# Loading x first and summing the modulation on TensorE in the opening phase of a hybrid decoder layer

## The chip, the cores and the metric

The kernel runs on one core of a Trainium2 chip. The metric is the time of one execution on the device in microseconds (us); smaller is better. The engines are named as in the profile: PE (TensorE matmuls) with PEld (its weight loads), DVE (VectorE), ACT (ScalarE), POOL (GpSimd) and SP (SyncE, which issues the DMAs here).

## The reference, cut to what matters

One layer of a decoder: a mixing sub-layer (pooling channels and dilated window attention) and a gated MLP, both modulated by a conditioning vector `c`. SEQ and D_MODEL are 1024, one sequence, all in f32. The change concerns the very first part: the norm of `x`, its modulation by the first 2048 columns of `c_act @ w_ada` (shift and scale), and the start of the input projection.

```python
c_act = jax.nn.silu(c)
mod = c_act @ w_ada[l] + b_ada[l]
sh_m, sc_m, gt_m, sh_f, sc_f, gt_f = (t[:, None, :] for t in jnp.split(mod, N_MOD, axis=-1))
h = rms_norm(x, g_pre_mix[l]) * (1.0 + sc_m) + sh_m
y = mixing_sublayer(h, cos, sin, w_in[l], w_pool[l], b_pool[l], pool_scale[l], w_out[l])
...
# in mixing_sublayer
proj = h @ w_in
...
q = partial_rope(qkv[:, :, 0], cos, sin) * (HEAD_DIM ** -0.5)
```

`cos` and `sin` come from the token positions.

## The kernel before, in words

`x` lies in eight tiles `xt[0]` to `xt[7]` of 128 tokens by 1024 features. The projection needs h with the features on the partitions, so h is made in eight chunks of 128 features: `turn` (L356) transposes one chunk of the tiles into the PSUM banks 6 and 7, and `h_chunk` (L404) applies scale and shift as per-partition columns while it copies them out on ACT. A product in f32 is made of three matmuls of reduced width: `hh` is the high part of h, `hl` the low part (`low`, L410), `wh` and `wl` those of a weight piece (`piece`, with `split` at L118 and L170). `proj(kc, 0)` is the high part of h times both parts of the weights (L399, L400), `proj(kc, 1)` the low part times the high weights (L396). In this first phase six of the eight token tiles (`NS`) go through the projection of the first attention unit chunk by chunk, each with a PSUM bank of its own; the last two tiles follow together (`turn_rest` L367, `h_rest` L374, `l_rest` L382).

The modulation columns of chunk kc come from a block `wa[kc]` of `w_ada`, 128 x 8 x 256 in f32, 1 MB. `mods` on DVE multiplies its eight 256-wide parts by the eight columns of `cact` and adds them up, two running sums in `acc` (L335 the first products, L339 the multiply-adds, L342 the sum of the two). `colsum` (L346) sums over the partitions on PE: two matmuls with `acc` as weights and a column of ones. `columns` (L350, L352) turns the result into the columns `acol` and `bcol`.

The norm: `norm_a` squares a tile with its sum on ACT (L315) and takes the root (L147), `norm_b` refines it and scales the tile in place (L325 on DVE; L323 on ACT for the tiles in `ON_ACT`). `angles` makes the angles on DVE and the sines on ACT (L243, L244). `warm` issues matmuls of a matrix of ones into a spare bank (L361).

The order on PE, ACT, DVE and POOL is written out by hand in this phase (`manual_schedule`): each engine runs its instructions in the order of the calls. The DMAs go out on SP in the order of `START`, as far as `loads` is called: a is a block of modulation weights, x a tile, w a weight piece of the first unit, i the identity and other early constants, m the masks. `wa` has three buffers, weight pieces two (`raw`), `acc` two. Before the loop, the modulation of block 0 and the norm of the first six tiles are done, in pairs (`NB`). Step kc of the loop over chunks 1 to 7 transposes chunk kc, sums its modulation over the partitions, prepares that of kc + 1 on DVE, makes h of chunk kc and projects chunk kc - 1. The norm of tiles 6 and 7 stands in step `NRM` = 6. After this phase only PE's order is written by hand; ACT's and DVE's is the scheduler's, which has put two weight pieces of the next unit into step 6.

Of the kernel before, what the change touches and what calls it, by code (L numbers as in the profile page):

```python
# [19 lines left out]
NK = D // P  # L20
# [50 lines left out]
NCONST = _const_layout()  # L71
LAST_X = (8, 6)
TURN_AT = ((5, 4, 0, 0), (6, 2, 0, 1), (6, 7, 1, 0), (7, 2, 1, 1), (8, 3, 2, 0), (8, 7, 2, 1), (9, 7, 3, 0), (10, 3, 3, 1))
START = "a0 x0 i0 x1 x2 x3 x4 x5 w0 a1 w1 a2 a3 w2 a4 a5 w3 a6 a7 x6 x7 m0"
WARM = (5, 5, 5)
NB = 2
NRM = 6
RT = 3
SPL = 3
MU = 2  # L80
# [19 lines left out]
def block_kernel(ctx: ExitStack, tc: tile.TileContext, x, pos, cols, rows, consts, w_ada_a, w_ada_b, w_in_u,  # L100
                 w_in_p, w_pool, w_out, w_up, w_down, out):
    nc = tc.nc
# [42 lines left out]
    def root(ssq, n=1, scale=1.0 / D):  # L145
        sd = sp.tile([P, n], F32, name="sd", tag="sm_sd")
        nc.scalar.activation(sd, ssq, AF.Sqrt, bias=epst, scale=scale)  # L147
        return sd
# [19 lines left out]
    def split(raw, wh, wl, hi_eng=None, lo_eng=None):  # L168
        copy(hi_eng or nc.scalar, wh, raw)
        (lo_eng or nc.vector).tensor_tensor(wl, raw, wh.bitcast(F32), ALU.subtract)  # L170
# [63 lines left out]
    def angles():  # L234
        nc.vector.tensor_copy(posf, posi)
        nc.vector.tensor_tensor(ang, posf[:, :, None].to_broadcast([P, NT, 8]),
                                cl("freq")[:, None, :].to_broadcast([P, NT, 8]), ALU.mult)
        nc.vector.tensor_scalar(turns, ang, INV_2PI, MAGIC, op0=ALU.mult, op1=ALU.add)
        nc.vector.tensor_scalar(turns, turns, MAGIC, None, op0=ALU.subtract)
        for part in _two_pi_parts():  # L240
            nc.vector.scalar_tensor_tensor(ang, turns, -part, ang, op0=ALU.mult, op1=ALU.add)
        nc.vector.tensor_scalar(ang, ang, 3.1415925, -3.1415925, op0=ALU.min, op1=ALU.max)
        nc.scalar.activation(sin, ang, AF.Sin)  # L243
        nc.scalar.activation(cos, ang, AF.Sin, scale=0.5)  # L244
        nc.vector.tensor_mul(cos, cos, cos)
        nc.vector.tensor_scalar(cos, cos, -2.0, 1.0, op0=ALU.mult, op1=ALU.add)

# [44 lines left out]
    with tc.tile_pool(name="st", bufs=2) as st:  # L292
        wa, raws = [], []

        def load(what, i):
            if what == "x":
                nc.sync.dma_start(xt[i], xv[:, i])
            elif what == "i":
                nc.sync.dma_start(cst[:, :early], consts[:, :early])
            elif what == "m":  # L300
                nc.sync.dma_start(cst[:, early:], consts[:, early:])
            elif what == "w":
                raws.append(load_raw(w_in_u[0, :, 2 * i:2 * i + 2, :], 768))
            else:
                w = st.tile([P, 8, 256], F32, name="wa", tag="wa", bufs=3)
                nc.sync.dma_start(w, w_ada_a[i])
                wa.append(w)

        ws, accs = [], {}
# [3 lines left out]
        def norm_a(t, n=1):  # L313
            for i in range(n):
                nc.scalar.activation(hl[7], xt[t + i], AF.Square, accum_out=ssq[:, t + i:t + i + 1])  # L315
            roots[t] = root(ssq[:, t:t + n], n)

        def norm_b(t, n=1):
            r0, v = rsqrt_parts(ssq[:, t:t + n], roots[t], n)
            for i in range(n):  # L320
                if (t, i) in ON_ACT:
                    nc.vector.tensor_scalar_mul(v[:, i:i + 1], v[:, i:i + 1], r0[:, i:i + 1])
                    nc.scalar.activation(xt[t + i], xt[t + i], AF.Copy, scale=v[:, i:i + 1])  # L323
                else:
                    nc.vector.tensor_scalar(xt[t + i], xt[t + i], r0[:, i:i + 1], v[:, i:i + 1], op0=ALU.mult,  # L325
                                            op1=ALU.mult)

        def mods(kc, part):
            if kc >= NK:
                return  # L330
            w = wa[kc]
            if part == 0:
                accs[kc] = st.tile([P, 2, 256], F32, name="acc", tag="acc", bufs=2)
                for i in range(2):
                    nc.vector.tensor_scalar_mul(accs[kc][:, i], w[:, 4 * i], cact[:, 4 * i:4 * i + 1])  # L335
            for j in ((1,), (2, 3))[part]:
                for i in range(2):
                    kb = 4 * i + j
                    nc.vector.scalar_tensor_tensor(accs[kc][:, i], w[:, kb], cact[:, kb:kb + 1], accs[kc][:, i],  # L339
                                                   op0=ALU.mult, op1=ALU.add)  # L340
            if part:
                nc.vector.tensor_add(accs[kc][:, 0], accs[kc][:, 0], accs[kc][:, 1])  # L342

        def colsum(kc):
            for i in range(2):
                nc.tensor.matmul(PS[:, 7, 256 + i:257 + i], accs[kc][:, 0, i * P:(i + 1) * P], ones[:, 0:1],  # L346
                                 start=True, stop=True)

        def columns(kc):
            nc.vector.tensor_scalar(acol[:, kc:kc + 1], PS[:, 7, 257:258], bsc1[:, kc:kc + 1], cl("g_pre_mix", kc),  # L350
                                    op0=ALU.add, op1=ALU.mult)
            nc.vector.tensor_add(bcol[:, kc:kc + 1], PS[:, 7, 256:257], cl("b_ada", kc))  # L352
# [29 lines left out]
                nc.vector.tensor_tensor(o[:, :, NS * P:], h32[:, i:i + n], hh[:, k:k + n, NS * P:].bitcast(F32),  # L382
                                        ALU.subtract)

        def piece(j):
            wh = wp.tile([P, 768], F32R, name="wh", tag="wh")
            wl = wp.tile([P, 768], F32R, name="wl", tag="wl")
            split(raws[j], wh, wl)
            ws.append((wh, wl))

        def proj(kc, part, ts_=range(NS)):
# [9 lines left out]

        def h_chunk(kc):
            h32 = st.tile([P, NS * P], F32, name="h32", tag="h32")
            nc.scalar.activation(h32, PS[:, 6:8, :].rearrange("p a b -> p (a b)")[:, 0:NS * P], AF.Identity,  # L404
                                 bias=bcol[:, kc:kc + 1], scale=acol[:, kc:kc + 1])
            copy(nc.scalar, hh[:, kc, 0:NS * P], h32)
            return h32

        def low(kc, h32):
# [2 lines left out]
        with tc.manual_schedule(engines={ET.PE, ET.Activation, ET.DVE, ET.Pool}):  # L412
            order = START.split()
            at = [0]

            def loads(n):
                for _ in range(n):
                    if at[0] < len(order):
                        load(order[at[0]][0], int(order[at[0]][1]))
                        at[0] += 1  # L420

            loads(order.index("a3"))
            angles()
            root(epst)
            for part in range(2):
                mods(0, part)
            colsum(0)
            for t in range(0, NS, NB):
                norm_a(t, NB)
                norm_b(t, NB)  # L430
                turn(0, range(t, t + NB))
                if t == 0:
                    columns(0)
                warm(WARM[t // 2])
            mods(1, 0)
            piece(0)
            h32 = h_chunk(0)
            mods(1, 1)
            low(0, h32)
            for kc in range(1, NK):  # L440
                loads((2, 3)[kc % 2])
                turn(kc, range(NS))
                if kc == 1:
                    proj(0, 0, range(SPL))
                colsum(kc)
                if kc == 1:
                    proj(0, 0, range(SPL, NS))
                mods(kc + 1, 0)
                columns(kc)
                if kc == NRM:  # L450
                    norm_a(NS, 2)
                h32 = h_chunk(kc)
                if kc > 1:
                    proj(kc - 1, 0)
                mods(kc + 1, 1)
                if kc == NRM:
                    norm_b(NS, 2)
                low(kc, h32)
                if kc in (1, 3, 5):
# [1003 lines left out]
```

## Time and profile before

| | us |
|---|---|
| median of 3 runs | 1079.86 (1079.12 to 1080.65) |
| the profiled execution | 1080.04 |
| its span, first to last instruction | 1078.3 |
| PE busy in the span | 1038.9 (96%) |
| DVE busy | 860.6 (80%) |
| ACT busy | 474.8 (44%) |
| mean granted TensorE clock | 0.99 |

The span is what the profile covers; the execution's own time has some 1.7 us around it. Busy shares are means over stages with different limits: the phase that is changed covers about the first 60 us.

### The profile page before, as it was taken

The numbers are of one execution on the slowest core, as the hardware profiler recorded it, in microseconds if no ns is written. First come the engines' busy times: TensorE is split into PE (matmuls) and PEld (weight loads), VectorE is DVE, ScalarE is ACT, GpSimd is POOL, SyncE is SP. The second block draws the span as 40 slices with busy tenths as digits, with TensorE's granted clock in tenths as the row PEclk, the third lists the DMA queues.
The fourth block names the chain that finished last, engine by engine and source line by source line (L and its number), as shares of the span: only waits on it lengthen the run. The fifth ranks groups of instructions, "written<-read, shape, count | busy, mean of one in ns | idle before, by whom it ended". The sixth has DMA issues, their size and how long they took to land.

```text
span 1078.3 us, 15477 instructions
## 1 busy us (share of the span) xinstructions
PE 1038.9 (96%) x5174; PEld 876.9 (81%) x5174; DVE 860.6 (80%) x1886; ACT 474.8 (44%) x958; POOL 217.9 (20%) x132
## 2 busy tenths in 40 slices
PE   4899999999999999999999999999999999999996
PEld 4898988898888877777888888888878888888885
DVE  8975466885457779999999888979789999756997
ACT  6564332433354469534433333432223455544541
POOL 0000000000000000063433333323235525003360
PEclk9999999999999999999999999999999999999999
DMA  9652346353131163323344424344434889566653
GB/s 361 212 154 74 114 112 193 94 174 91 53 94 51 30 235 137 118 88 131 120 160 140 164 100 155 118 150 163 166 117 138 287 290 383 161 196 207 225 173 117
DMA packets 85148, 168.34 MB, mean 156 GB/s; under 512 B 9158, under 2 KB 25926, under 8 KB 81356
## 3 DMA queue, kind: packets, MB, share of 16 engines
q1 hardware_dynamic: 85068, 167.35, 46.7%
q8 instruction: 41, 0.67, 0.3%
q14 instruction: 39, 0.32, 0.1%
HBM read 134.47 MB, written 32.84 MB: 155 GB/s over the span
## 4 chain that ended last, share of the span: by engine, by line
PE 73%; DVE 16%; DMA 5%; ACT 3%; issue 2%; SPq 0%; POOL 0%; DVEq 0%; ACTq 0%; POOLq 0%
PE PS L1044 9%; PE PS L1045 9%; PE PS L1046 9%; PE PS L1345 6%; PE PS L1344 6%; PE PS L1346 6%; PE PS L222 5%; PE PS L224 5%; PE PS L223 5%; PE PS L685 3%; PE PS L655 2%; DMA gm<-in_w_ada_b_dram 2%; DMA mraw<-in_w_ada_b_dram 2%; PE PS L675 1%; DVE more L1119 1%
## 5 line engine op out<-in xcount | busy, mean ns | idle before, releaser
L1123 POOL TENSOR_TENSOR raws<-rw 128x512 f32<-128x512 f32 x30 | 45.5, 1516 | 512.5 <-DVE t2r L1068 450.3
L222 PE MATMUL PS<-wh,hh 128*128 128x384 f32 x336 | 125.4, 373 | 0.0
L224 PE MATMUL PS<-wh,hl 128*128 128x384 f32 x336 | 113.9, 339 | 0.0
L223 PE MATMUL PS<-wl,hh 128*128 128x384 f32 x336 | 113.7, 338 | 0.0
L118 ACT ACTIVATE more<-raws 128x512 fp32r<-128x512 f32 x81 | 49.6, 624 | 67.0 <-PE PS L1045 53.1
L1119 DVE TENSOR_TENSOR more<-raws,more 128x512 fp32r<-128x512 f32 x75 | 71.7, 958 | 3.1 <-ACT more L118 3.1
L664 ACT ACTIVATE pm<-pm,nm 128x128 f32<-128x128 f32 (+1 forms) x96 | 42.4, 443 | 65.0 <-DVE nm L662 43.8
L222 PEld LDWEIGHTS PS<-wh,hh 128*128 128x128 f32 x336 | 64.0, 190 | 7.9 <-issue 4.8
L223 PEld LDWEIGHTS PS<-wl,hh 128*128 128x128 f32 x336 | 64.0, 191 | 0.6 <-issue 0.5
L224 PEld LDWEIGHTS PS<-wh,hl 128*128 128x128 f32 x336 | 63.7, 189 | 0.0
L1064 ACT ACTIVATE cv<-GG,col 128x1024 f32<-128x1024 f32 x22 | 27.4, 1245 | 76.0 <-DVE GG L1063 76.0
L1044 PE MATMUL PS<-a,more 128*128 128x512 f32 x144 | 56.1, 390 | 1.3 <-DVE VV L1060 1.3
L1046 PE MATMUL PS<-a,more 128*128 128x512 f32 x144 | 56.3, 391 | 1.0 <-DVE more L1119 1.0
L1045 PE MATMUL PS<-a,more 128*128 128x512 f32 x144 | 56.0, 389 | 0.0
L658 DVE CUSTOM_DVE_ANT_0 pm<-PS,cst 128x128 f32<-128x128 f32 (+1 forms) x96 | 30.8, 348 | 29.7 <-PE PS L655 22.6
L1345 PE MATMUL PS<-tail 128*128 128x512 f32 x128 | 49.9, 390 | 0.0
L1344 PE MATMUL PS<-tail 128*128 128x512 f32 x128 | 49.8, 389 | 0.0
L1346 PE MATMUL PS<-tail 128*128 128x512 f32 x128 | 49.8, 389 | 0.0
L1158 ACT ACTIVATE cv<-cv 128x1024 f32<-128x1024 f32 x22 | 23.4, 1062 | 57.9 <-DVE cv L1156 57.9
L1154 DVE SCALAR_TENSOR_TENSOR cv<-GG,col,cv 128x1023 f32<-128x1023 f32 x22 | 36.9, 1678 | 11.4 <-ACT cv L1064 11.4
L170 DVE TENSOR_TENSOR wl<-raw,wh 128x768 fp32r<-128x768 f32 (+1 forms) x34 | 34.8, 1033 | 12.0 <-ACT wh L118 11.8
L489 DVE SCALAR_TENSOR_TENSOR macc<-mraw,cact,macc 128x512 f32<-128x512 f32 x42 | 31.4, 748 | 15.6 <-DMA mraw<-in_w_ada_b_dram 15.4
(389 smaller groups left out, 3102.5 us busy)
## 6 DMA issues: line engine op xcount, KB each, us to landing
rw<-in_w_up_dram SPq DMA_DIRECT2D x21, 1024.0 KB
gscr<-VV SPq DMA_DIRECT2D x66, 256.0 KB
mraw<-in_w_ada_b_dram SPq DMA_DIRECT2D x48, 256.0 KB
R<-in_w_down_dram SPq DMA_DIRECT2D x48, 256.0 KB
raw<-in_w_in_u_dram SPq DMA_DIRECT2D x24, 384.0 KB
wa<-in_w_ada_a_dram SPq DMA_DIRECT2D x8, 1024.0 KB
R<-gscr SPq DMA_DIRECT2D x27, 256.0 KB
raws<-in_w_up_dram SPq DMA_DIRECT2D x25, 256.0 KB
```

What stands on the lines that cost most here:

```text
L118: nc.scalar.activation(o, i, AF.Copy)
L222: nc.tensor.matmul(o, a, wh[:, c0:c0 + 384], start=k == 0, stop=False)
L223: nc.tensor.matmul(o, a, wl[:, c0:c0 + 384], start=False, stop=False)
L224: nc.tensor.matmul(o, b, wh[:, c0:c0 + 384], start=False, stop=k == 7)
L1044: nc.tensor.matmul(o, wh[:, ks], ah, start=k == 0, stop=False)
L1045: nc.tensor.matmul(o, wh[:, ks], al, start=False, stop=False)
L1046: nc.tensor.matmul(o, wl[:, ks], ah, start=False, stop=k == 3)
L1119: nc.vector.tensor_tensor(wl, r, wh.bitcast(F32), ALU.subtract)
L1123: nc.gpsimd.tensor_tensor(t, a, b, ALU.add)
L1344: nc.tensor.matmul(o, gh[:, ts_], wh, start=k == 0, stop=False)
L1345: nc.tensor.matmul(o, gh[:, ts_], wl, start=False, stop=False)
L1346: nc.tensor.matmul(o, gl[:, ts_], wh, start=False, stop=k == KD - 1)
```

## The change

- `START`: the first x tile goes ahead of modulation block 0, which is now loaded in two halves behind the sixth x tile; tiles 6 and 7 move ahead of block 3. The first call loads 14 entries, each later step as many as `LOADS` says.
- `ON_PE` gives for each block how many of its eight parts are multiplied and summed on PE directly, with the block's 128 x 128 squares as weights and columns of `cact` as the moving operand. For block 0 it is all eight, and nothing is left on DVE; block 1 has four, block 2 two, block 4 four, the others none.
- `mods_first`: the two first products of what remains move from DVE to ACT (for block 1 they stay on DVE).
- Piece 0's high part is made on DVE, behind the columns of chunk 0. Chunk 0's `hh` is written straight from PSUM, ahead of `h32`.
- In step 1 the first half of the projection of chunk 0 stands ahead of the transposes.
- The norm of tiles 6 and 7 moves from step 6 to step 3, the sines (with ACT's table) from the start to step 5, the cosines on DVE with them. The third block of warm-up matmuls goes.

```diff
-START = "a0 x0 i0 x1 x2 x3 x4 x5 w0 a1 w1 a2 a3 w2 a4 a5 w3 a6 a7 x6 x7 m0"
-WARM = (5, 5, 5)
+START = "x0 i0 x1 x2 x3 x4 x5 a0 w0 a1 w1 a2 x6 x7 a3 w2 a4 w3 a5 a6 a7 m0"
+FIRST_LOADS, LOADS = 14, (0, 2, 2, 1, 1, 1, 1, 0)
+ON_PE = (8, 4, 2, 0, 4, 0, 0, 0)
+TRIG_AT = 5
+WARM = (5, 5, 0)
 NB = 2
-NRM = 6
+NRM = 3
...
+        def mods_first(kc, eng):
+            if kc >= NK or ON_PE[kc] == 8:
+                return
+            accs[kc] = st.tile([P, 2, 256], F32, name="acc", tag="acc", bufs=2)
+            for i in range(2):
+                kb = ON_PE[kc] + i
+                if eng is nc.scalar:
+                    nc.scalar.activation(accs[kc][:, i], wa[kc][:, kb], AF.Copy, scale=cact[:, kb:kb + 1])
+                else:
+                    nc.vector.tensor_scalar_mul(accs[kc][:, i], wa[kc][:, kb], cact[:, kb:kb + 1])
...
         def mods(kc, part):
...
+            kbs = range(ON_PE[kc] + 2, 8)
+            for j, kb in enumerate(kbs):
+                if (j > 1) == part:
+                    nc.vector.scalar_tensor_tensor(accs[kc][:, j % 2], wa[kc][:, kb], cact[:, kb:kb + 1],
+                                                   accs[kc][:, j % 2], op0=ALU.mult, op1=ALU.add)
...
         def colsum(kc):
+            n = ON_PE[kc]
             for i in range(2):
-                nc.tensor.matmul(PS[:, 7, 256 + i:257 + i], accs[kc][:, 0, i * P:(i + 1) * P], ones[:, 0:1],
-                                 start=True, stop=True)
+                o, c = PS[:, 7, 256 + i:257 + i], slice(i * P, (i + 1) * P)
+                for kb in range(n):
+                    nc.tensor.matmul(o, wa[kc][:, kb, c], cact[:, kb:kb + 1], start=kb == 0, stop=kb == 7)
+                if n < 8:
+                    nc.tensor.matmul(o, accs[kc][:, 0, c], ones[:, 0:1], start=n == 0, stop=True)
...
-            loads(order.index("a3"))
+            loads(FIRST_LOADS)
+            root(epst)
             angles()
-            root(epst)
-            for part in range(2):
-                mods(0, part)
-            colsum(0)
             for t in range(0, NS, NB):
                 norm_a(t, NB)
+                if t == NS - NB:
+                    colsum(0)
                 norm_b(t, NB)
                 turn(0, range(t, t + NB))
-                if t == 0:
-                    columns(0)
                 warm(WARM[t // 2])
+            columns(0)
+            piece(0, nc.vector)
+            h32 = h_chunk(0)
+            mods_first(1, nc.vector)
+            low(0, h32)
             mods(1, 0)
-            piece(0)
-            h32 = h_chunk(0)
             mods(1, 1)
-            low(0, h32)
             for kc in range(1, NK):
-                loads((2, 3)[kc % 2])
-                turn(kc, range(NS))
+                loads(LOADS[kc])
                 if kc == 1:
                     proj(0, 0, range(SPL))
+                turn(kc, range(NS))
                 colsum(kc)
                 if kc == 1:
                     proj(0, 0, range(SPL, NS))
+                mods_first(kc + 1, nc.scalar)
                 mods(kc + 1, 0)
                 columns(kc)
...
                 if kc > 1:
                     proj(kc - 1, 0)
+                if kc == TRIG_AT:
+                    sines()
                 mods(kc + 1, 1)
                 if kc == NRM:
                     norm_b(NS, 2)
                 low(kc, h32)
+                if kc == TRIG_AT:
+                    cosines()
```

More of the change, by code (lines that the diff above doesn't have):

```diff
@@ L242, in angles, with sines, cosines @@
         nc.vector.tensor_scalar(ang, ang, 3.1415925, -3.1415925, op0=ALU.min, op1=ALU.max)
+    def sines():
         nc.scalar.activation(sin, ang, AF.Sin)
         nc.scalar.activation(cos, ang, AF.Sin, scale=0.5)
+    def cosines():
         nc.vector.tensor_mul(cos, cos, cos)
@@ L305, in load @@
                 w = st.tile([P, 8, 256], F32, name="wa", tag="wa", bufs=3)
-                nc.sync.dma_start(w, w_ada_a[i])
+                if i:
+                    nc.sync.dma_start(w, w_ada_a[i])
+                else:
+                    for j in (0, 4):
+                        nc.sync.dma_start(w[:, j:j + 4], w_ada_a[i, :, j:j + 4])
                 wa.append(w)
@@ L326, in norm_b @@
                                             op1=ALU.mult)
+        def mods_first(kc, eng):
[6 more added lines that the diff above has]
+                    nc.scalar.activation(accs[kc][:, i], wa[kc][:, kb], AF.Copy, scale=cact[:, kb:kb + 1])
+                else:
+                    nc.vector.tensor_scalar_mul(accs[kc][:, i], wa[kc][:, kb], cact[:, kb:kb + 1])
         def mods(kc, part):
-            if kc >= NK:
+            if kc >= NK or ON_PE[kc] == 8:
                 return
[L331 to L340, printed above, removed]
+            kbs = range(ON_PE[kc] + 2, 8)
[3 more added lines that the diff above has]
+                                                   accs[kc][:, j % 2], op0=ALU.mult, op1=ALU.add)
             if part:
@@ L383, in l_rest, with piece @@
                                         ALU.subtract)
-        def piece(j):
+        def piece(j, eng=None):
             wh = wp.tile([P, 768], F32R, name="wh", tag="wh")
             wl = wp.tile([P, 768], F32R, name="wl", tag="wl")
-            split(raws[j], wh, wl)
+            split(raws[j], wh, wl, hi_eng=eng)
             ws.append((wh, wl))
@@ L403, in h_chunk @@
             h32 = st.tile([P, NS * P], F32, name="h32", tag="h32")
-            nc.scalar.activation(h32, PS[:, 6:8, :].rearrange("p a b -> p (a b)")[:, 0:NS * P], AF.Identity,
-                                 bias=bcol[:, kc:kc + 1], scale=acol[:, kc:kc + 1])
-            copy(nc.scalar, hh[:, kc, 0:NS * P], h32)
+            src = PS[:, 6:8, :].rearrange("p a b -> p (a b)")[:, 0:NS * P]
+            if kc == 0:
+                nc.scalar.activation(hh[:, kc, 0:NS * P], src, AF.Identity, bias=bcol[:, kc:kc + 1],
+                                     scale=acol[:, kc:kc + 1])
+            nc.scalar.activation(h32, src, AF.Identity, bias=bcol[:, kc:kc + 1], scale=acol[:, kc:kc + 1])
+            if kc:
+                copy(nc.scalar, hh[:, kc, 0:NS * P], h32)
             return h32
```

## The prediction

> **What bounds the kernel now.** I read the page first (engine rows in 40 slices of 27 us), then busy time in stretches, then the timeline of the first 60 us.
>
> ```profile
> PE   4899999999999999999999999999999999999996
> DVE  8975466885457779999999888979789999756997
> ```
>
> PE is short of work in the first two slices alone; DVE is at 8 and 9 there. The stretches (us, then busy time of PE, PEld, DVE, ACT, POOL, granted clock, DMA share, GB/s) say the same:
>
> ```profile
> 20.00:58.00 38.00, 33.49 (x195) 29.68 (x196) 36.01 (x93) 20.42 (x26) 0.00 (x0) 0.96 0.65 238
> 66.00:130.00 64.00, 64.00 (x401) 59.84 (x400) 36.30 (x145) 27.89 (x76) 0.00 (x0) 1.00 0.42 124
> ```
>
> From 20 to 58 us DVE is nearly full; from 66 to 130 us PE has no idle time, and the page's slices of PE stay at 9 from the third on. So whatever moves the moment at which PE stops waiting, near 57.45 us (the transposes of the last two tiles, L367), should move the end by as much. One step of the first phase on DVE, start by start:
>
> ```profile
> 32.75 0.61 DVE L335 TENSOR_SCALAR acc<-wa,cact 128x256 f32<-128x256 f32 x2
> 33.28 0.87 DVE L339 SCALAR_TENSOR_TENSOR acc<-wa,cact,acc 128x256 f32<-128x256 f32 x2
> 34.07 0.27 DVE L350 TENSOR_SCALAR acol<-PS,bsc,col 128x1 f32<-128x1 f32 x1
> ...
> 34.33 1.66 DVE L339 SCALAR_TENSOR_TENSOR acc<-wa,cact,acc 128x256 f32<-128x256 f32 x4
> 36.02 0.43 DVE L342 TENSOR_TENSOR acc<-acc 128x256 f32<-128x256 f32 x1
> 36.40 0.96 DVE L410 TENSOR_TENSOR hl<-h,hh 128x768 fp32r<-128x768 f32 x1
> 37.28 0.95 DVE L170 TENSOR_TENSOR wl<-raw,wh 128x768 fp32r<-128x768 f32 x1
> 38.15 0.61 DVE L335 TENSOR_SCALAR acc<-wa,cact 128x256 f32<-128x256 f32 x2
> ```
>
> Differences of starts are the prices: two first products 0.53, a multiply-add 0.41, columns 0.26, joining add 0.38, low part 0.88, a weight piece 0.87. The step takes 5.40 us with a piece, 4.53 without. The same on PE:
>
> ```profile
> 34.63 1.21 PE L396 MATMUL PS<-wh,hl 128*128 128x384 f32 x6
> 35.68 0.82 PE L356 MATMUL PS<-cst,xt 128*128 128x128 f32 x6
> 36.50 0.61 PE L346 MATMUL PS<-onesr,acc 128*128 128x1 f32 x4
> 36.97 0.42 PE L399 MATMUL PS<-wh,hh 128*128 128x384 f32 x1
> ...
> 39.13 1.21 PE L396 MATMUL PS<-wh,hl 128*128 128x384 f32 x6
> ```
>
> Six low-part matmuls 1.05, six transposes 0.82, a column sum 0.47 for four instructions (0.117 each; two per call, as the inputs are f32), twelve high-part matmuls 2.16: 4.50 us a step. PE therefore has little room of its own: 0.9 us in a step with a piece, nothing in one without.
>
> **The change part by part.**
>
> DVE. In steps 1 to 6 it loses six pairs of first products (3.2 us, now on ACT) and six multiply-adds (four of block 2 and 4 each counted against six before, so 2 + 4, 2.5 us): 5.7 us. DVE stops being the bound.
>
> PE. Matmul calls of the column sums go from 2 per block to 16, 10, 6, 2, 10, 2, 2, 2. Blocks 1 to 7 have 68 instructions where there were 28. The price of a longer run, warm and at half clock:
>
> ```profile
> 183.84 1.87 PE L519 MATMUL PS<-onesr,macc 128*128 128x1 f32 x8 [0.85 <-DVE macc L489]
> 185.57 0.67 PE L222 MATMUL PS<-wh,hh 128*128 128x384 f32 x1
> ```
>
> ```profile
> 217.48 0.95 PE L519 MATMUL PS<-onesr,macc 128*128 128x1 f32 x8
> 218.29 0.42 PE L222 MATMUL PS<-wh,hh 128*128 128x384 f32 x1
> ```
>
> 0.81 for eight is 0.101 each; 1.73 for eight, at half clock as shown below, is 0.216. I take 0.107, between 0.101 and 0.117. Block 0 alone is then 32 x 0.107 = 3.4 us (3.2 to 3.7). That these accumulate into one PSUM column is not in the trace; the high-part pairs accumulate in one bank without a gap, so I add nothing.
>
> The start. Its rows in the timeline, and a stretch with the DMA rate:
>
> ```profile
> 13.63 2.34 PE L361 MATMUL PS<-onesr 128*128 128x128 f32 x10
> 14.40 1.06 ACT L315 ACTIVATE hl<-xt 128x1024 fp32r<-128x1024 f32 x1
> 16.28 1.28 PE L361 MATMUL PS<-onesr 128*128 128x128 f32 x10
> 18.32 0.44 PE L356 MATMUL PS<-cst,xt 128*128 128x128 f32 x2 [0.76 <-ACT xt L323]
> 18.91 0.97 ACT L404 ACTIVATE h<-PS,bcol,acol 128x768 f32<-128x768 f32 x1
> 20.81 0.44 PE L399 MATMUL PS<-wh,hh 128*128 128x384 f32 x1
> 57.45 1.09 PE L367 MATMUL PS<-cst,xt 128*128 128x128 f32 x8 [0.88 <-ACT h L404]
> ```
>
> ```profile
> 10.00:15.00 5.00, 3.01 (x13) 2.63 (x14) 3.98 (x15) 4.87 (x11) 0.00 (x0) 1.00 1.05 429
> ```
>
> The first weight block is 1.05 MB; at 429 GB/s the x tiles come 2.45 us earlier, and the sixth tile's square moves from 14.40 to 11.9. But block 0 now lands where that tile did, up to 14.4, and its column sum stands on PE behind the second warm-up block, which moves from 16.28 to 13.8 and ends at 15.1 (warm) to 16.1 (cold). So the sum runs from 15.1-16.1 to 18.5-19.5, with 0.27 of transposes behind it. The columns on DVE now wait for this sum, and behind them stand weight piece 0 on DVE and the chunk h on ACT. After the columns (0.26) come the high copy of weight piece 0 (new there; between 0.53, two 256-wide products, and 0.87; I take 0.7) and its low part 0.87; the chunk's high part, now written straight from PSUM, is ready by then. First projection matmul: 20.6 to 21.8, I take 21.2, against 20.81. The 2.45 us gained by the x tiles are eaten by the 3.4 us of block 0.
>
> From there PE has, up to the L367 transposes: seven sets of transposes 5.7, seven high parts 15.1, six low parts 6.3, column sums 68 x 0.107 = 7.3, together 34.4. 21.2 + 34.4 = 55.6; with 1 us of waits, 56.6. Before, from 20.81, the work was 29.6 (one set of transposes was already done, sums 3.3) in 36.6 us: 7.0 idle or at half clock. At an unchanged clock this is 57.45 - 56.6 = 0.9 us gained.
>
> The small moves. The norm of tiles 6 and 7 goes ahead of block 3's modulation on ACT (two squares and a root, 2.4 us); PE still has 2.16 of high parts to run then, so I charge at most 1 us, the wait above. Sines and their table go to step 5. ACT's cover, and the table's row:
>
> ```profile
> ACT h L404 <- DVE bcol L352: 14.7, 5, 3.8
> 5.93 1.28 ACT L147 ACT_TABLE_LOAD   x1
> L374 ACT ACTIVATE wa<-PS,bcol,acol 128x256 f32<-128x256 f32 x8 | 3.8, 560 | 0.0
> ```
>
> ACT waited 14.7 us in five waits, 2.9 a step. It now takes two products of 256 columns (at most 1.1 by L374) and once 1.28 for the table plus some 0.5 for the sines: 2.9, just covered. Without that cover the cosines, and the weight piece behind them on DVE, wait up to 1 us. [...] The row shows 1.28, and the sum goes by the row. The third warm-up block, ten instructions, goes; at its place PE works on block 0. SP issues one DMA more (block 0 in halves, 0.4 us, behind all x tiles that matter). Tiles 6 and 7 go ahead of block 3, whose buffer now comes free only when PE ends block 0; it is wanted two steps later, some 8 us, against 2.5 us of transfer. Loads of pieces 2 and 3 queue on SP behind such waits with as much room. Nothing charged.
>
> The clock. Stretches of 3.41 us between the moments at which the granted clock changed:
>
> ```profile
> 12.86:16.27 3.41, 3.16 (x14) 2.67 (x14) 3.27 (x13) 2.92 (x8) 0.00 (x0) 1.00 1.05 437
> 29.93:33.34 3.41, 2.73 (x18) 2.17 (x17) 3.38 (x9) 1.84 (x2) 0.00 (x0) 1.00 0.67 199
> 50.41:53.82 3.41, 2.13 (x15) 1.90 (x15) 3.38 (x11) 2.21 (x3) 0.00 (x0) 1.00 0.25 54
> 53.82:57.23 3.41, 2.75 (x9) 2.24 (x8) 2.42 (x8) 1.98 (x2) 0.00 (x0) 0.50 0.67 209
> 183.52:186.93 3.41, 3.09 (x12) 3.09 (x13) 3.41 (x22) 1.53 (x7) 0.00 (x0) 0.50 0.45 138
> 186.93:190.34 3.41, 3.41 (x13) 2.88 (x14) 1.44 (x12) 0.71 (x5) 0.00 (x0) 0.50 0.54 154
> ```
>
> After a stretch with PE at 2.13 the clock fell to 0.50 for a whole stretch; after one at 2.73 it held. The fifth row matters most: PE was busy for 3.09 of 3.41, and the clock stayed at 0.50 through the next stretch too. In it the one-column matmuls ran until 185.57. The warm-up's 128-wide ones, in the first row with 3.16, brought the clock up (2.34 for ten, then 1.28; the records start with the first change, so the column reads 1.00 there). So one-column matmuls do not seem to count as work. [...]
>
> In the changed kernel PE does nothing wide from 15.1-16.1 to 20.6-21.8, 5.6 us. However stretches of 3.41 fall on that, one has at least 2.8 us of it, so under 0.6 us of wide work: the clock should fall. Block 1's sum (transposes 0.82, then 20 instructions, 2.1 us or 4.3 at half clock) keeps it low or fells it again. A stretch of steady work at half clock loses 1.7 us. One, partly idle, would cost 0.8; three 5.1. I take two: 3.4.
>
> Sum: -0.9 + 3.4 = +2.5 us. Against the profiled execution's 1080.04 (span 1078.3) that is 1082.5; the median of the runs, 1079.86, is 0.18 below it: 1082.4. A change of 0.2%, 2.16 us, is about what timing can tell from none.
>
> **The rivals.**
> Clock holds, PE full: one-column matmuls count after all (the weight loads beside them are full-size, PEld 3.09 in the fifth row). Then -0.9: 1079.0. Against it: that row.
> Faster: the clock holds and PE runs without a wait, since DVE and ACT have room: start 20.6, work at 0.101 33.9, L367 at 54.5, 3.0 us earlier: 1076.9. It decides from L367 before 55.2. For it: DVE's 5.7 us. Against: the norm in step 3 and the table in step 5 stand ahead of what PE needs.
> Clock low for long: block 0's sum runs at 0.216 (6.9 us instead of 3.4), block 4 (2.96 us without wide work) fells it a third time: +5, 1084.9.
>
> **How the numbers follow.** Clock falls for about two stretches: 0.48, own range 1080.7 to 1084.4, a third of it within 0.2%. Clock holds: 0.25. Faster: 0.15. Clock low for long: 0.12. So faster 0.15; same 0.25 + 0.15 = 0.40; slower 0.33 + 0.12 = 0.45. The range 1077.0 to 1085.2 takes in the rivals' times and leaves out the outer half of the faster case and a third of the last.
>
> **What would show it.** Right: L335 gone from DVE after step 1, DVE with idle time in the steps; L346 with 100 instructions, 0.107 warm; the first L399 near 21; granted clock 0.50 in one or more stretches between 17 and 32 us; L367 near 60. Wrong: clock at 1.00 throughout the steps, L367 before 57; or PE waiting on block 3 or 4's load, which I charged at nothing; or a changed pattern of half-clock stretches after 180 us, where a shift of the work could gain or lose one.

## The result, and the profile after

The changed kernel takes 1093.21 us (median of six runs, 1087.60 to 1094.67) against 1079.58 (six runs, 1078.28 to 1080.65): ratio 1.0115, 95% interval 1.0090 to 1.0141. The forecast was 1082.4, range 1077.0 to 1085.2: the direction was right, but 13.6 us were lost where 2.5 were forecast. The profiled execution is the quickest of the six: 1087.60, span 1085.8.

The page's rows after, 40 slices of 27 us:

```profile
PE   4999999999999998989999999999999999999996
DVE  5676455986366879999999888878789999756897
PEclk8899999999999999989999999999999999999999
```

DVE is relieved in the first two slices, as meant, and PE looks busier than before. The third row takes the gain back: the granted clock is at 8 in both (9 in both before). Busy time in stretches of 3.41 us, cut where the clock changed, and the stretch that was shown of before (us, then busy time of PE, PEld, DVE, ACT, POOL, granted clock, DMA share, GB/s):

```profile
16.03:19.44 3.41, 3.41 (x33) 3.41 (x32) 1.52 (x5) 1.15 (x1) 0.00 (x0) 1.00 1.03 428
19.44:22.85 3.41, 2.96 (x14) 2.55 (x14) 0.41 (x3) 0.00 (x0) 0.00 (x0) 0.50 0.99 416
22.85:26.26 3.41, 2.34 (x7) 2.16 (x8) 3.36 (x7) 2.66 (x4) 0.00 (x0) 0.50 1.05 436
26.26:29.67 3.41, 3.41 (x19) 3.41 (x17) 1.49 (x4) 0.00 (x0) 0.00 (x0) 0.50 0.38 150
29.67:33.09 3.42, 3.42 (x15) 3.42 (x15) 1.42 (x5) 0.99 (x1) 0.00 (x0) 0.50 0.27 53
33.09:36.50 3.41, 3.41 (x13) 3.31 (x13) 2.66 (x5) 2.37 (x4) 0.00 (x0) 0.50 0.63 257
36.50:39.91 3.41, 3.41 (x27) 3.41 (x26) 1.95 (x7) 1.38 (x2) 0.00 (x0) 1.00 0.64 183
20.00:58.00 38.00, 36.48 (x209) 35.67 (x210) 26.17 (x65) 22.44 (x35) 0.00 (x0) 0.78 0.58 221
```

Five stretches in a row stand at 0.50; a sixth follows at 63.80. DVE fell from 36.01 to 26.17 us between 20 and 58. The first row is the one to learn from: PE was busy for all of its 3.41 us, and the clock fell at its end. What it did, in the same view for the one-column matmuls alone (PE, PEld, clock, DMA share, GB/s), first in that stretch, then in the fourth:

```profile
16.03:19.44 3.41, 2.30 (x22) 2.41 (x22) 1.00 1.03 428
...
26.26:29.67 3.41, 2.05 (x10) 2.24 (x10) 0.50 0.38 150
```

2.30 of the 3.41 us were one-column matmuls, and so were 2.05 of a later full stretch that did not bring the clock back. On the timeline of PE:

```profile
12.46 0.47 PE L377 MATMUL PS<-cst,xt 128*128 128x128 f32 x1 [12.46 <-DVE xt L336]
...
16.01 1.29 PE L382 MATMUL PS<-onesr 128*128 128x128 f32 x10
17.14 4.73 PE L366 MATMUL PS<-cact,wa 128*128 128x1 f32 x32
21.73 0.67 PE L377 MATMUL PS<-cst,xt 128*128 128x128 f32 x2
23.92 0.69 PE L420 MATMUL PS<-wh,hh 128*128 128x384 f32 x1 [1.52 <-ACT hh L427]
...
61.22 0.87 PE L377 MATMUL PS<-cst,xt 128*128 128x128 f32 x6 [1.21 <-ACT h L429]
62.92 0.61 PE L368 MATMUL PS<-onesr,acc 128*128 128x1 f32 x4 [0.82 <-DVE acc L359]
67.01 1.15 PE L388 MATMUL PS<-cst,xt 128*128 128x128 f32 x8
```

The last two tiles' transposes, at 57.45 before, come 9.56 us later, while the span grew by 7.5. This is the quickest of the six runs; the same kernel's profile in e9, at 1093.56 near the median, has them 10.5 us later and 3.0 us more behind them. And the x tiles, though loaded first, bring almost nothing. ACT after:

```profile
0.73 1.28 ACT L150 ACT_TABLE_LOAD   x1 [0.73 <-PEq L1481]
...
2.34 1.28 ACT L197 ACT_TABLE_LOAD   x1
...
7.84 1.06 ACT L326 ACTIVATE hl<-xt 128x1024 fp32r<-128x1024 f32 x1 [1.42 <-DMA xt<-in_x_dram]
8.80 0.19 ACT L326 ACTIVATION_READ_ACCUMULATOR hl<-xt 128x1 f32 x1
9.00 1.28 ACT L150 ACT_TABLE_LOAD   x1
10.30 0.29 ACT L150 ACTIVATE sd<-ssq,epst 128x2 f32<-128x2 f32 x1
...
55.61 1.28 ACT L248 ACT_TABLE_LOAD   x1
```

Before, the second tile's square stood at 9.30; now at 7.84. But the root behind it waits for a table that had been loaded once already: the early `root(epst)` (L150, load at 0.73) now runs ahead of silu (L197), which loads its own table over it at 2.34, and the first true root pays 1.28 us at 9.00. PE's first transpose moves from 12.64 to 12.46 only.

Over all experiments the runs of the changed kernel reach from 1081.06 to 1094.67, those of before from 1076.60 to 1084.50. Part of that comes from the moments at which the clock changed, which lie differently to the program from run to run: the first fall is at 19.44 us in this profile and at 21.04 in that of the first experiment. One execution of e8 below took 2040.59 us and is left out of its median and its ratio.

### The profile page after: what moved, and what is told of

It reads as the page before. It is cut to its first block, busy times and chain, and to the rows that moved or that the text cites. A ratio compares the mean times of both kernels' runs of the same rounds, so it can differ in the third digit from the quotient of the medians.

```text
span 1085.8 us, 15587 instructions
## 1 busy us (share of the span) xinstructions
PE 1045.1 (96%) x5232; PEld 886.6 (82%) x5232; DVE 850.5 (78%) x1856; ACT 482.2 (44%) x971; POOL 220.4 (20%) x132
## 4 chain that ended last, share of the span: by engine, by line
PE 62%; DVE 20%; DMA 9%; ACT 4%; issue 4%; SPq 0%; DVEq 0%; POOL 0%; ACTq 0%; POOLq 0%
PE PS L1073 8%; PE PS L1075 8%; PE PS L1074 8%; PE PS L1374 6%; PE PS L1375 6%; PE PS L1373 6%; DMA mraw<-in_w_ada_b_dram 4%; PE PS L225 4%; PE PS L227 3%; PE PS L226 3%; PE PS L714 2%; DVE more L1148 2%; DMA gm<-in_w_ada_b_dram 2%; PE PS L684 1%; DVE cv L1183 1%
## 5 line engine op out<-in xcount | busy, mean ns | idle before, releaser
L518 DVE SCALAR_TENSOR_TENSOR macc<-mraw,cact,macc 128x512 f32<-128x512 f32 x42 | 31.5, 749 | 16.5 <-DMA mraw<-in_w_ada_b_dram 16.1
## 6 DMA issues: line engine op xcount, KB each, us to landing
rw<-in_w_up_dram SPq DMA_DIRECT2D x21, 1024.0 KB
wa<-in_w_ada_a_dram SPq DMA_DIRECT2D x7, 1024.0 KB
```

## The experiments

The measured values together. "Stretches" are those of 3.41 us at half clock in the first 70 us of the profile, from the granted clock by tens of us; "L388" is the start of the last two tiles' transposes there, whatever its line in that kernel. The runs come from several chips, and each ratio is to runs of the kernel before beside them (medians 1080.54 for e1 to e4, 1080.74 for e5 to e8, 1079.91 for e9 to e12); it is not the quotient of the two medians.

| kernel | L388 | stretches | median us | ratio to before |
|---|---|---|---|---|
| before | 57.45 | 1 | 1079.58 | |
| changed | 67.01 | 6 | 1093.21 | 1.0115 (1.0090 to 1.0141) |
| e1 changed again | 62.52 | 3 | 1081.06 | one run |
| e2 wide moving operand | 63.05 | 1 | 1085.08 | 1.0041 (1.0025 to 1.0058) |
| e3 silu first | 66.79 | 6 | 1089.95 | 1.0082 (1.0062 to 1.0101) |
| e4 both | 60.16 | 1 | 1085.15 | 1.0027 (1.0000 to 1.0055) |
| e5 old start, new steps | 58.19 | 1 | 1082.02 | 1.0018 (1.0002 to 1.0033) |
| e6 the same, no sums on PE | 56.98 | 1 | 1080.94 | 1.0005 (0.9986 to 1.0024) |
| e7 new start, old steps | 62.62 | 5 | 1084.51 | 1.0052 (1.0030 to 1.0073) |
| e8 first products on ACT | 54.37 | 0 | 1076.57 | 0.9984 (0.9963 to 1.0006) |
| e9 changed again | 67.99 | 6 | 1091.30 | 1.0098 (1.0072 to 1.0124) |
| e10 warm-up behind the sum | 62.99 | 3 | 1085.24 | 1.0057 (1.0035 to 1.0080) |
| e11 first products, again | 54.40 | 0 | 1076.68 | 0.9973 (0.9957 to 0.9990) |
| e12 norm split | 54.28 | 0 | 1078.21 | 0.9981 (0.9966 to 0.9996) |

**e1: the changed kernel, unedited.**

> The changed kernel once more, nothing edited, for a second trace. Its runs spread from 1087.6 to 1094.7, those of before from 1078.3 to 1080.7. Theory (the granted clock): the one-column matmuls of the block sums leave stretches of 3.41 us without wide work; how many fall depends on where the stretches begin, so this trace shows half clock in a different set of them. If its time is near 1094, the half-clock time before the last-tile transposes (L388) is 5 to 7 us longer than the 20 us of the first trace and L388 starts 3 to 6 us after 67.0. Rival (the spread comes from later parts, where ACT and DVE are ordered anew): the first 70 us agree within 1 us, and the difference stands after 180 us.

Its windows, the second from the transposes alone (PE, PEld, clock, DMA share, GB/s), and its timeline:

```profile
21.04:24.45 3.41, 1.89 (x9) 1.40 (x9) 1.99 (x6) 1.59 (x2) 0.00 (x0) 0.51 1.02 422
24.45:27.87 3.42, 3.42 (x16) 3.32 (x15) 3.27 (x8) 1.07 (x3) 0.00 (x0) 0.50 0.90 376
...
24.45:27.86 3.41, 1.48 (x6) 1.30 (x6) 0.50 0.90 377
```

```profile
17.91 3.94 PE L366 MATMUL PS<-cact,wa 128*128 128x1 f32 x32
...
62.52 1.03 PE L388 MATMUL PS<-cst,xt 128*128 128x128 f32 x8
```

The same instructions at nearly the same places (first projection at 23.90 against 23.92) met the clock's boundaries 1.6 us later (21.04 against 19.44). It came back after two stretches in place of five, and PE was through 4.49 us earlier. That refutes the rival, by which the first 70 us would agree within 1 us. e1's third stretch, at 45 us, came elsewhere: block 4's sum fell whole into the stretch before it, which in the changed kernel's trace divided it between two stretches. So the difference at L388 is three stretches, 1.5 us each.

**e2: the same sums, with a moving operand of 128 equal columns.**

```diff
-nc.tensor.matmul(o, wa[kc][:, kb, c], cact[:, kb:kb + 1], ...)
+nc.tensor.matmul(o, wa[kc][:, kb, c], cact[:, kb:kb + 1].to_broadcast([P, P]), ...)
```

The sum over the partitions behind it gets 128 columns of ones likewise.

> The changed kernel with the moving operand of every block-sum matmul broadcast to 128 columns instead of one: same number of matmuls and weight loads, same sums. Theory (clock): the 128-wide warm-up matmuls took 0.12 us each and brought the clock up, so the sums now count as work. No half clock between 20 and 45 us, L388 near 59 instead of 67.0, 1079 to 1082 us, spread under 2 us. Rival (the extra PE work and the later start cost the time by themselves, the low clock only covers waits): L388 stays at 65 or later, time above 1086.

```profile
18.93 3.74 PE L366 MATMUL PS<-cact,wa 128*128 128x128 f32 x32
...
63.05 1.07 PE L388 MATMUL PS<-cst,xt 128*128 128x128 f32 x8
```

```profile
20.00:30.00 10.00, 8.42 (x64) 7.76 (x64) 6.08 (x16) 3.05 (x5) 0.00 (x0) 1.00 0.88 332
30.00:40.00 10.00, 10.00 (x70) 9.94 (x69) 8.14 (x21) 8.40 (x15) 0.00 (x0) 1.00 0.86 321
```

With the same 32 weight loads, the same order and the same quiet time between columns and chunk 0, the clock holds from 20 to 40 us. So the width of the moving operand is what the clock missed, not idle time. All profiles agree: in the six with block 0's one-column sum (after, e1, e3, e7, e9, e10) the clock fell between 19.2 and 21.1 us; in the two with 128 columns (e2, e4) it did not, and stood at 1.00 from 10 to 40 us. It costs hardly more: 3.74 / 32, 0.117 an instruction, against 0.101 for one column at full clock (e5). The ratio falls from 1.0115 to 1.0041 (8 us; from 1.0098 on the chip of e9, 6 us), but these are different chips, and the one run of the changed kernel on e2's chip is e1's 1081.06, below all of e2's (1084.23 to 1087.11). The comparison on one chip is e3 against e4 below, where the width is the only difference. The expectation's 59 for L388 and 1079 to 1082 were both missed. What is left, 4.4 us, is no clock of the opening: the sum starts at 18.93, and steps 5 and 6 wait as in the changed kernel (1.39 and 0.82 us).

**e3 and e4: silu ahead of the root, alone and with e2's edit.**

```diff
-    nc.scalar.activation(cact, cl("c"), AF.Silu)
...
+            nc.scalar.activation(cact, cl("c"), AF.Silu)
             root(epst)
```

> The changed kernel with the silu of c issued ahead of the first root on ACT, so that ACT loads its tables twice at the start and not three times (silu, root; not root, silu, root). In the trace of the changed kernel the third load stands at 9.00 us between the second square and the first root. Theory (it holds the norm): first transposes 1.3 to 2 us earlier than 12.46, block 0's sum 1 to 2 us earlier than 17.14, and the time 1 to 2 us less if the clock falls as before; 1086 to 1093. Rival (block 0's load holds its sum, or the clock's stretches hide the gain): the start of block 0's sum moves by less than 0.5 us or the time stays within the spread.

> Both edits together: 128-column moving operands in the block sums, and the silu ahead of the first root. Theory (clock and table load are the two things that cost the time): L388 near 57.5 to 58.5, 1077.5 to 1081, level with the kernel before or up to 2 us below it. Rival (the start is held by block 0's load): no different from the wide moving operand alone. Rival (PE's added work costs the time): above 1085.

The third table load, at 9.00, is gone in both. In e3 the second x tile's square stood at 8.92, later than in the changed kernel, so its first transpose gained 0.20 only. In e4 the square stood at 7.84 and the start shows what the load had hidden:

```profile
11.19 0.47 PE L376 MATMUL PS<-cst,xt 128*128 128x128 f32 x1 [11.19 <-DVE xt L335]
...
15.98 3.74 PE L365 MATMUL PS<-cact,wa 128*128 128x128 f32 x32
...
60.16 1.03 PE L387 MATMUL PS<-cst,xt 128*128 128x128 f32 x8
```

L388 is 2.89 us earlier than in e2, 0.94 of it from the tile's arrival (8.78 in e2). The medians of e2 and e4 do not differ, though: in the profiled runs the part behind L388 took 1024.0 us in e4 and 1019.8 in e2. That the load costs its 1.28 us in the opening is shown; that it costs the total anything is not, and the theory's 1077.5 to 1081 was missed.

e3 and e4 also show what the width is worth in the total: all four runs of e4 (1079.20 to 1085.95) are below all four of e3 (1087.67 to 1091.37), the medians 4.8 us apart. L388 is 6.6 us earlier, 1.1 of it from the tile's arrival.

**e5, e6, e7: the opening and the steps apart.** e5 takes the opening of before (block 0 first and on DVE, silu first, three warm-up blocks) and keeps the new steps; e6 is e5 without sums on PE; e7 takes the new opening and the old steps. e7's opening is not quite the changed kernel's: silu and the sines stand ahead of the first root, so the third table load is gone, and step 1's transposes stand ahead of the first projection again.

```diff
-ON_PE = (8, 4, 2, 0, 4, 0, 0, 0)
+ON_PE = (0, 4, 2, 0, 4, 0, 0, 0)   # e5;  e6: all 0;  e7: (8, 0, 0, 0, 0, 0, 0, 0)
```

> The changed kernel with the opening as before (block 0 loaded first and summed on DVE, silu ahead of the root, three warm-up blocks, piece 0 as before); its steps stay (one-column sums of 4, 2 and 4 parts for blocks 1, 2 and 4, first products on ACT, norm of tiles 6 and 7 in step 3, sines in step 5). Theory clock, opening: the quiet stretch in front of the first projection is what fells the clock. Then it holds or falls once, at block 1 or block 4; the last two tiles' transposes start at 54 to 58 us, the first projection matmul near 20.8, total 1077 to 1081. Rival, steps: the one-column sums of the steps and the crowded steps 5 and 6 cost as much as the opening. Then two or more stretches at half clock between 24 and 60 us, the transposes at 60 to 64, total 1083 to 1089.

> As the previous one, but no part of any block is multiplied on TensorE: all multiply-adds on DVE, the first products of blocks 2 to 7 on ACT, norm of tiles 6 and 7 in step 3, sines in step 5. Theory clock: without one-column runs no stretch falls under what holds the clock, so full clock from 17 us to the last two tiles' transposes, which start at 54.5 to 57; total 1076.5 to 1080. Rival, steps: the moved norm and sines make ACT late in steps 3 and 5, waits of 0.8 to 1.4 us in each: transposes at 58 to 60, total 1081 to 1083, whatever the clock does.

> The changed kernel with its new opening (x tiles first, block 0 summed whole on TensorE, silu behind the root, sines at the start), and the steps of before: blocks 1 to 7 on DVE, first products too, norm of tiles 6 and 7 in step 6. Theory clock, opening: the 32 one-column matmuls fell the clock as in the changed kernel, at 19 to 21 us, for two to five stretches of 3.41; first projection matmul at 22.5 to 24.5, the last two tiles' transposes at 62 to 67, total 1084 to 1092. Rival, steps: without the one-column sums of blocks 1, 2 and 4 the clock comes back after one stretch, and the transposes start at 58.5 to 60.5, total 1080 to 1083.

e5's timeline and window, then e7's:

```profile
21.92 0.95 PE L361 MATMUL PS<-cact,wa 128*128 128x1 f32 x8
22.73 0.36 PE L363 MATMUL PS<-onesr,acc 128*128 128x1 f32 x2
...
52.28 0.88 PE L372 MATMUL PS<-cst,xt 128*128 128x128 f32 x6 [1.42 <-ACT h L424]
```

```profile
20.00:30.00 10.00, 9.95 (x73) 9.83 (x73) 7.21 (x18) 5.64 (x10) 0.00 (x0) 1.00 0.98 385
```

```profile
16.91 4.45 PE L366 MATMUL PS<-cact,wa 128*128 128x1 f32 x32
...
24.30 1.54 PE L377 MATMUL PS<-cst,xt 128*128 128x128 f32 x6 [2.40 <-ACT h L429]
```

In e5 block 1's 20 one-column instructions between wide work leave the clock at 1.00 through 50 us in the profiled run. Its late loss is step 5's (1.42, chunk h late behind the sines' table, 1.28 us at 46.67). So the steps alone cost 0.18%, 1.9 us; L388 and the median are just outside the theory's ranges. The opening alone, e7, costs 0.52%, 5.6 us, with the clock down from about 20 to 33 us; its profile is of the slowest of its eight runs (1090.14; the others 1082.81 to 1086.42). L388 and the median are in its theory's ranges, and the last of its five stretches began behind L388; but the first projection, at 25.49, is 1 us behind it, since step 1's transposes now stand ahead of it and wait 2.40 us for chunk 0. Together they cost 0.98% to 1.15%, 3 to 5 us more than the sum. With intervals of 1.6 to 2.8 us on either side of each ratio, and e7's opening without the third load, this excess is uncertain. e10 shows a way in which the two add up. e6 went between its two theories: the norm in step 3 together with the first products on ACT made PE wait 2.25 us for chunk h at 42.19, and the clock fell once there (0.83 from 40 to 50 us); L388 at 56.98, the total as before.

**e8 and e11: the kernel before, with only the first products moved to ACT.**

```diff
-nc.vector.tensor_scalar_mul(accs[kc][:, i], w[:, 4 * i], cact[:, 4 * i:4 * i + 1])
+if kc > 1: nc.scalar.activation(accs[kc][:, i], w[:, 4 * i], AF.Copy, scale=cact[:, 4 * i:4 * i + 1])
```

> The kernel before with one edit: the first products of blocks 2 to 7 on ACT in place of DVE. DVE loses 0.53 us in each of six steps, which is 3.2 us; PE and the opening are untouched. Theory: DVE was the bound of the steps, the clock holds as before, so the last two tiles' transposes start at 54.3 to 55.7 in place of 57.45, the total is 1076.5 to 1078.5. Rival, ACT in the way: its cover of 2.9 us a step is cut by the wait for the weight block, chunk h comes later, and nothing is gained: transposes at 57 to 58, total 1079.5 to 1081. Rival, alignment: the total is moved by a stretch of half clock gained or lost after 180 us, 1.7 us either way, with the transposes still at 54.3 to 55.7.

> The kernel before with the first products of blocks 2 to 7 on ACT, once more in more rounds. Theory: the last two tiles' transposes stay near 54.4 us against 57.45 and the time follows; the ratio to the kernel before is 0.9965 to 0.9985, and its interval ends below 1. Rival: the 3 us are given back in part by half-clock stretches later on, whose place depends on when the work comes; ratio 0.999 to 1.000.

```profile
54.37 1.09 PE L370 MATMUL PS<-cst,xt 128*128 128x128 f32 x8 [1.07 <-ACT h L407]
```

3.08 us earlier than before in e8, 3.05 in e11, with no stretch at half clock up to there (1.00 in every 10 us from 10 to 70): DVE was the bound of the steps, and this one part of the change frees it without taking anything from the clock. Before, the stretch from 53.82 with its 2.75 us of work at half clock followed PE's waits on DVE and ACT; its loss, an estimated 1.4 us, is part of the 3. The first interval includes 1; the second, 0.9957 to 0.9990, does not. This version beats both kernels, the one before by 2.9 us by e11's ratio (1.7 by e8's).

**e9 and e10: the changed kernel again, and with a warm-up block behind block 0's sum.**

```diff
-WARM = (5, 5, 0)
+WARM = (5, 5, 5)
```

> The changed kernel once more, beside the next three. Theory alignment: the moments at which the clock can change stand in no fixed relation to the program, so its runs spread with the number of half-clock stretches in the first 70 us, from three (1081) to six (1088) or more: runs from 1081 to 1095, median 1086 to 1093, and a profile whose loss in the opening goes with its count of stretches. Rival: the slower first measurement was of that chip alone; then this one stays within 1080 to 1085 throughout.

> The changed kernel with one edit: the third block of ten 128-wide warm-up matmuls is put back, which stands behind the one-column sum of block 0 and ahead of the first projection, where TensorE waits some 2 us anyway. Theory: the sum still fells the clock at 19 to 21 us, but the ten matmuls (2.1 us at half clock) bring the stretch around the first projection over what restores it, so the clock is back by 26 to 28 us in every alignment: the last two tiles' transposes at 60.5 to 63.5, total 1080 to 1086, with a smaller spread than the kernel without them. Rival: block 1's one-column sum and the waits of step 1 decide; then half clock up to 33 us or more as before, transposes at 64 to 67, total 1086 to 1094.

e9's runs went from 1088.34 to 1093.56: the slowness is no matter of one chip. e1's 1081.06 was not met again among them. In e10 the ten wide matmuls filled the 1.5 us that PE waits there in the changed kernel:

```profile
17.67 4.04 PE L366 MATMUL PS<-cact,wa 128*128 128x1 f32 x32
...
22.04 2.34 PE L382 MATMUL PS<-onesr 128*128 128x128 f32 x10
```

```profile
26.00:28.00 2.00, 2.00 (x13) 1.90 (x12) 1.59 (x4) 0.00 (x0) 0.00 (x0) 0.61 0.76 311
28.00:30.00 2.00, 2.00 (x18) 2.00 (x18) 0.20 (x2) 0.00 (x0) 0.00 (x0) 1.00 0.04 13
30.00:32.00 2.00, 2.00 (x11) 2.00 (x10) 1.35 (x5) 1.74 (x2) 0.00 (x0) 0.74 0.65 193
32.00:34.00 2.00, 2.00 (x11) 1.91 (x10) 1.87 (x3) 1.63 (x4) 0.00 (x0) 0.50 0.79 332
```

By these clocks it was back at 27.6 us and fell once more at 31.0: the stretch between held block 1's sum. L388 came at 62.99, and the total is below e9's on the same chip, by 6 us in the medians and 4.4 by the ratios. The warm-up itself is work for nothing, and still it pays. A smaller spread is not shown: e10's runs reach from 1084.92 to 1089.20.

**e12: e11 with the norm of tiles 6 and 7 spread over steps 5 and 6.**

```diff
-                if kc == NRM:
-                    norm_a(NS, 2)
+                if kc in (NRM - 1, NRM):
+                    square(kc + 1)
                 h32 = h_chunk(kc)
+                if kc == NRM:
+                    roots[NS] = root(ssq[:, NS:NS + 2], 2)
```

> The previous kernel with the norm of tiles 6 and 7 spread: the square of tile 6 in step 5 and that of tile 7 in step 6, each in ACT's gap of 1.3 us ahead of chunk h; the root behind chunk h of step 6; tiles 6 and 7 loaded two and one entries earlier, block 7 one tile later. Theory: TensorE's waits of 1.43 and 1.07 us on chunk h in steps 6 and 7 are ACT's late squares; one or both go, the transposes of the last two tiles start at 52.0 to 53.5, and the time is 0.8 to 2.4 us under the previous kernel's. Rival: the next unit's weight pieces, which the scheduler places, move into the freed gaps or block 7 comes late; the waits stay and the transposes start at 54 to 55.

```profile
54.28 1.09 PE L373 MATMUL PS<-cst,xt 128*128 128x128 f32 x8 [1.96 <-ACT h L410]
```

The rival held: the wait of step 6 went, and came back as 1.96 us on chunk h of step 7. Nothing gained over e11.

## Why the prediction was wrong

**The clock, the step that failed.** "I take two: 3.4" was the mis-sized term. The mechanism stood: one-column matmuls did not count as work in the way that wide ones did (granted clock from 20 to 30 us 1.00 in e2 and e4, 0.50 in e3 and the changed kernel). But the stretches were six in the profiled run, where I had two, and the term came to some 7.9 us there (the 3.4, and the 1.2 and 3.3 found below). Five came from the block sums; the sixth, at 63.80, followed the waits of steps 5 and 6, as one at 53.82 did before. I had asked only what fells the clock, and given one stretch at half clock for each quiet time. In these profiles more work stood in the stretches that brought it back than in the leanest that held it. The eleven profiles with a stretch at half clock show it up to 70 us, when the wide matmuls and the transposes of each stretch are added up, each from its start to the next one's. Of the stretches at half clock, 17 had 2.57 us or less and were followed by another; 17 had 2.76 or more and full clock came back. At full clock, the 17 behind which it fell had 1.70 or less, while the lowest that held had 1.50 and 1.57, with 1.9 us of one-column matmuls beside. So a stretch with block 1's sum in it held a full clock (e1, from 27.90: 1.57), and another did not bring a low one back (the changed kernel, from 29.67: 1.63). In which stretch a sum falls depends on the boundaries, which only a spread could have covered. "Clock low for long", my rival at 0.12, named the right course, and at 1084.9 was too small as well. That e1's 1081.06 lies near the forecast is luck of the boundaries, and of a part behind L388 that was 4.1 us shorter than before.

**The start, also wrong.** First projection at 21.2 forecast, 23.92 measured, 2.7 us late. 1.5 of it: block 0's sum began at 17.14, where I took 15.1 to 16.1. The second tile's square came 1.46 us earlier, where I had 2.45, and the third table load took 1.28 us of it back; without the load, in e4, the sum began at 15.98. I had counted the tables of the moved sines and not the order of root and silu. 1.2 more: the sum took 4.59 us up to the next instruction in place of 3.4, as the clock fell at 19.44 in its midst. What follows, columns to projection, took 2.2 us where I had 2.1, but that is luck: I had the two parts of weight piece 0 on DVE in this path and the chunk's high part ready by then, and the trace has the first projection waiting for that high part on ACT (1.52 <-ACT hh). Two slips of the working change little: by its own terms the upper end of the start is 21.6, not 21.8, and of the multiply-adds block 2 loses two and block 4 four, as the sum has it.

**The steps.** From 23.92 to 67.01 are 43.1 us; the forecast was 34.4 of work, 1 of waits and 3.4 of clock, 38.8, so 4.3 more. Waits of 1.21 and 0.82 in steps 5 and 6 make 2.0 where 1 was allowed. DVE, then ACT, in step 5:

```profile
58.07 0.96 DVE L173 TENSOR_TENSOR wl<-raw,wh 128x768 fp32r<-128x768 f32 x1 [0.28 <-ACT wh L121]
```

```profile
53.72 0.99 ACT L429 ACTIVATE h<-PS,bcol,acol 128x768 f32<-128x768 f32 x1 [1.34 <-DVE bcol L373]
...
60.17 0.99 ACT L429 ACTIVATE h<-PS,bcol,acol 128x768 f32<-128x768 f32 x1 [0.60 <-DVE bcol L373]
```

The table holds up the weight piece on ACT, that its low part on DVE, and that the columns and chunk h: the path named for the case that the cover is gone. Ahead of step 5's chunk ACT had 1.34 us to spare, where 2.9 less 1.1 was counted. The 0.82 is block 7's joining add, behind a piece of the next unit on DVE. The other 3.3 is left for the clock; this is a remainder, not a measurement. The price of a stretch, 1.7, was near: e1 gives 1.5.

**Right.** DVE freed and no longer the bound but in steps 5 and 6; the price of a one-column matmul (e5: eight in 0.81 at full clock, 0.101 each); no wait for a block's load; the direction, and the reason for it. The late stretches were named as a risk: the pair from 183 us is gone after (clock 1.00 from 180 to 200), and the part behind L388 was 2.1 us shorter in that run. In e9 the part behind L388 was 3.0 us longer than before instead, so this term has either sign. Over the profiles it reaches from 1016.8 (e1) to 1025.8 us (e7): the premise that a shift of L388 moves the end by as much holds only to some 4 us in a single run.

**Open.** What moves the part behind L388 by up to 9 us between profiles; why e1 alone among the eleven runs of this kernel came in at 1081; and whether opening and steps together exceed their sum, for which e10's second fall is one way shown, not the whole.

## What to carry to other kernels

The work moved here from a full engine to PE was paid for with PE's clock, five stretches in a row at 0.50: give such sums a wide moving operand (128 columns in e2, clock 1.00 from 20 to 40 us), or keep wide work within each stretch (e5, block 1's 20 one-column instructions, clock 1.00 from 20 to 50 us), and look at the granted clock before the busy share. With the clock held in the opening, the change still lost some 3 to 4 us by the ratios (e4, e2). Move one part at a time: the products on ACT alone gave 1.7 to 2.9 us, hidden in a change that lost 13. When an activation is moved, write down the order of table functions on ACT before and after: the third load took 1.28 us here.

## What was not expected of the hardware

- A PE that was busy for the whole of a stretch (3.41 of 3.41 us, 2.30 of it one-column matmuls) lost its clock: 1.00 in that stretch, 0.50 in the next five. With 128 columns in their place (e2) the clock stayed at 1.00 from 20 to 40 us.
- Transposes counted as work, by all that these traces show. In e1 the stretch from 24.45, with 1.48 us of transposes, 0.54 of one-column matmuls and 1.4 of others, brought the clock back (its row stands under e1); the changed kernel's from 22.85, with 2.14 of others and 0.20 of transposes, did not. The one-column matmuls of the first and the transposes of the second (PE, PEld, clock, DMA share, GB/s):

```profile
24.45:27.86 3.41, 0.54 (x4) 0.75 (x4) 0.50 0.90 377
```

```profile
22.85:26.26 3.41, 0.20 (x1) 0.42 (x2) 0.50 1.05 436
```

Others show the same: from start to start, three half-clock stretches with 1.49 to 1.94 us of other wide matmuls and 1.27 to 1.28 of transposes brought the clock back (one in e1, two in e10), while five with 2.11 to 2.17 and at most 0.46 did not (after, e3, e7, e9, e10). No run tested it by itself.
- The same kernel's two profiles (after, e1) differ by 4.49 us at L388 by the place of the clock's boundaries (19.44 and 21.04), with the first projection 0.02 us apart.
- The second x tile's square started at 7.84 to 8.92 us in four kernels with the same load order (after, e2, e3, e4), each time released by its load: some 1 us by arrival. PE's first transpose in the changed kernel itself, at 12.46, 12.45 (e1) and 13.43 (e9), moved as much.
